# Adaptive-norm products on four column tiles, tanh in place of silu and sigmoid, and a wider spread of fillers in a two-branch attention layer

## The chip, the cores and the metric

The kernel runs on one core of one Trainium2 chip. The metric is device time in microseconds (us) from start to end of one launch; the program gives the median of several runs. TensorE (PE in the profile) does the matmuls, VectorE (DVE), ScalarE (ACT) and GpSimd (POOL) do the elementwise work, and SyncE (SP) issues nearly all DMAs.

## What is computed

One encoder layer is applied to two independent sequences ("prompt", group 0, and "sample", group 1) of 1024 tokens with 1024 channels in float32. Both share all weights.

```python
mod = einsum(silu(c), w_ada) + b_ada            # [B, 3*1024]
shift, scale, gate = split(mod, 3)
h = rms_norm(x, norm_g) * (1 + scale) + shift
qa, ka, va, za, qb, kb, vb, zb, ga, gb = split(h @ w_in)   # 5376 columns
oa = gqa_attention(rope(rms(qa)), rope(rms(ka)), va) * silu(za)
ob = diff_attention(rope(rms(qb)), rope(rms(kb)), vb, lam)
ob = rms_norm(ob, subln_g) * (1 - lam_init) * silu(zb)
merged = sigmoid(ga) * (oa @ w_proj_a) + sigmoid(gb) * (ob @ w_proj_b)
out = x + gate * (merged @ w_out)
```

Branch A has 8 query heads of 64 on 2 key heads; branch B has 4 heads with two softmax maps each. `c` is one vector per group, so the product with `w_ada` has two rows only.

## The kernel before

Activations are kept transposed, 128 channels on the partitions, and the big products are made with operands split in a high and a low part of type fp32r (three products instead of one). A whole group is worked through before the next one.

**Start.** `start` (L338) loads the part of `w_ada` that makes shift and scale in eight tiles of 1 MB (`load_ada`, L244: 512 rows by 512 columns), group 0's `xT` in two halves of 512 tokens (`load_xT0`, 2 MB each) and the first projection weight, `kva_w` (1 MB, `early=True`). All of that goes through SP's queue in the order of the program text: two w_ada tiles, the first half of `xT`, three w_ada tiles, `kva_w`, three w_ada tiles, the second half of `xT`. `ada` (L293) runs four matmuls for each tile: the stationary operand is two columns of `silu(c)` (`cT`, [128, 8, 2]), the moving one 512 columns of `w_ada`, and all eight of a pair of tiles accumulate in two PSUM partitions. `ada_end` (L301) copies the two rows out, transposes them with the identity and adds the bias. `modulated` (L318) then makes the two parts of `h` for the first half. For the second half `squares` and `inv_rms` (L267) sum the squares over all channels with a matmul against ones, 8 chunks by 4 token tiles, in two passes each; `start_late` (L367) finishes that half from inside the head. `spread` puts its row of 1/rms into the one `ev` buffer, which the gates of `z_gen` use too.

**Head.** `head` (L957) makes k, v and the first half of q of branch A (`proj_tt`, L487: 24 matmuls of 256 columns for each of 8 token tiles), and lays gate products of `z_gen` (L668) between them. For group 0 it weaves 6 steps of `kva` with 3 of the gates, calls `late()`, and weaves 6 and 3 again.

**Gates.** `z_gen` makes za, zb, ga and gb: 24 matmuls of 512 columns for each [128, 512] block, one ACT copy out of PSUM into `ev`, one DMA to HBM (`zd`). There are 48 blocks a group. The silu is taken later in `gated_gen` (L848), where the block comes back beside the attention output (`od`); the sigmoid is taken in `merge_gen` (L892, L906).

**Attention.** `attention` (L808) gives out 32 units a group. A unit is four blocks of scores (L709, L710), a row maximum (L711, DVE), an exponential (L712, ACT), a 32x32 block transpose (L753, DVE) with four DMAs (L762) that finish it, and the product with the values (`a_values` L764 for branch A, two column tiles of 64 columns; `b_values` L780 for branch B, full width). All other work is woven between these steps as fillers. `weave` (L72) always takes a step from the stream with the smallest `steps done / steps given - lead`.

**Last head.** L1085 weaves the last head of branch B (44 steps, given as `LAST_ATT` = 48) with `fill()` (given as `LAST_FILL` = 28) and with `gated_gen` for the first three pairs of channel blocks (12 steps, `GATED_A` = -0.2, which makes it begin late). `fill` holds, for group 0, `gate_gen` (L427: the third part of `w_ada`, 16 matmuls with two stationary columns, each on a tile of 256 KB from the `st` pool of three), then the gate blocks that are left, and then ten of the sixteen steps of branch A's projection (`merge_gen`). After that come the rest of the projections and `out_gen`.

The framework places the instructions of each engine from a simulated timeline in order of priority, so the order on an engine is near the text's but not the same. A tile of a pool is any free one of its `bufs` buffers.

Of the kernel before, what the change touches and what calls it, by code (L numbers as in the profile page):

```python
# [20 lines left out]
P = 128  # L21
# [33 lines left out]
LAST_ATT, LAST_FILL = (48, 28)  # L55
# [4 lines left out]

SILU = 0
# [29 lines left out]
def kernel(ctx: ExitStack, tc: tile.TileContext, t: dict):  # L91
# [79 lines left out]
    nhalf = const.tile([P, 32], F32, name="nhalf")  # L171
    nc.vector.memset(nhalf, -0.5)


# [53 lines left out]
    ccol = const.tile([P, NCH, 2], F32, name="ccol")  # L228
# [5 lines left out]
    dma(ccol, t["c_col"])  # L234
# [23 lines left out]
    def added(sq):  # L258

        a, b = sq  # L260
        nc.vector.tensor_tensor(out=a[:, :2], in0=a[:, :2], in1=b[:, :2], op=ALU.add)
        nc.vector.tensor_tensor(out=a[:, 2:], in0=a[:, 2:], in1=b[:, 2:], op=ALU.add)
        nc.vector.tensor_tensor(out=a[:, :2], in0=a[:, :2], in1=a[:, 2:], op=ALU.add)
        nc.vector.tensor_tensor(out=a[:, 0], in0=a[:, 0], in1=a[:, 1], op=ALU.add)
        return [a[:, 0]]

    def inv_rms(sq):  # L267

        ps = gbank()
        for k in range(4):  # L270
            for i, x in enumerate(sq):
                nc.tensor.matmul(
                    ps[:, k : k + 1], x[:, k * P : (k + 1) * P], ones_c, start=(i == 0), stop=(i == len(sq) - 1)
                )
        ss = tiny.tile([P, 4], F32, tag="ss", name=nm("ss"))
# [17 lines left out]
    def ada(n, wt):  # L293
        hf, third, q = n // 4, n // 2 % 2, n % 2
        if q == 0:
            accs[n // 2] = gbank()[:2]
        acc = accs[n // 2]
        for c in range(4):
            nc.tensor.matmul(acc, cT[:, q * 4 + c], wt[:, c], start=(q == 0 and c == 0), stop=(q == 1 and c == 3))

    def ada_end(n):  # L301
        hf, third = n // 4, n // 2 % 2
        acc = accs[n // 2]
        row = halves2(ptile())[0][:2]
# [12 lines left out]

    def modulated(ht, hf, xT, cs):  # L318
        for c in cs:
            scale, shift = modc[:, 1, c, 0:1], modc[:, 0, c, 0:1]  # L320
            if c % 4 > 1:
                nc.scalar.activation(xT[c], xT[c], AF.Identity, scale=scale, bias=shift)
            else:
                nc.vector.tensor_scalar(
                    out=xT[c], in0=xT[c], scalar1=scale, scalar2=shift, op0=ALU.mult, op1=ALU.add
                )
            nc.scalar.activation(ht[hf][0][c], xT[c], AF.Copy)
            nc.vector.tensor_tensor(out=ht[hf][1][c], in0=xT[c], in1=ht[hf][0][c].bitcast(F32), op=ALU.subtract)
# [9 lines left out]
    def start(ht):  # L338
        nc.scalar.activation(cT, ccol, AF.Silu)
# [5 lines left out]
        wts += [load_ada(n) for n in range(2, 5)]  # L345
        kva_w.append(load_w(w_cols(w_in, (C_KA, 256)), early=True))
        wts += [load_ada(n) for n in range(5, 8)]
        xT.append(load_xT0(1))
        for n in range(8):
# [8 lines left out]
            if n == 4:  # L358
                split_early(kva_w[0])
                add_h(ht, 0, 0)  # L360
                modulated(ht, 0, xT[0], range(4))
        add_h(ht, 0, 1)
        modulated(ht, 0, xT[0], range(4, 8))
        rs = inv_rms([q[:, c] for q in squares(xT[1]) for c in range(4)])
        return lambda: start_late(ht, xT, rs)
# [31 lines left out]
    def load_tables_B():  # L397
# [19 lines left out]
        nc.vector.tensor_scalar(out=subg, in0=subg, scalar1=(1.0 - LAM_INIT) * math.sqrt(2 * HD), scalar2=None, op0=ALU.mult)  # L417
# [9 lines left out]
    def gate_gen():  # L427
        for half in range(2):
            acc = gbank()[:2]
            for k in range(NCH):  # L430
                st = spool.tile([P, 512], F32, tag="st", name=nm("st"))
                col = 2 * D + half * 512
                dma(st, w_ada[k * P : (k + 1) * P, col : col + 512])
                nc.tensor.matmul(acc, cT[:, k], st, start=(k == 0), stop=(k == NCH - 1))
                if k % 2:
                    yield 1
            row = rtile()[:2]
            nc.vector.tensor_copy(row, acc)
            ps = gbank()[:, :8].rearrange("p (c g) -> p c g", g=2)
            for c in range(4):  # L440
                nc.tensor.transpose(ps[:, c, :], row[:, c * P : (c + 1) * P], ident[:2, :2])
# [3 lines left out]
            )  # L445

# [39 lines left out]

    def proj_tt(ht, w, tt):  # L487
# [4 lines left out]
        for c in range(NCH):  # L492
            if c in CUTS:
                yield 1
            for lt, wi in ((hh, 0), (hh, 1), (hl, 0)):
                nc.tensor.matmul(ps, lt[c][:, sl], w[:, c, wi, :], start=(k == 0), stop=(k == 23))  # L496
# [54 lines left out]

    def behind(ins, other):
        dep = mybir.DependencyInfo(mybir.DependencyClass.NoSync, mybir.DependencyReason.DATA)
        tc.add_manual_dep(ins.ins, other.ins.name, dep)

    def together(calls):

        prev = None
        for call in calls:
            if prev is None:  # L560
                ins = call()
            else:
                with tc.high_priority(offset=TOP):
                    ins = call()
                behind(ins, prev)
            prev = ins
# [101 lines left out]
    def z_gen(ht, col, dst, i0, fn=AF.Copy):  # L668
        w = load_w(w_cols(w_in, (col, 256)))
        for hf in range(2):  # L670
            for e in range(2):
# [3 lines left out]
                for c in range(NCH):  # L675
                    if c in CUTS:
                        yield 1
                    for wi, rt in ((0, hh), (0, hl), (1, hh)):
                        nc.tensor.matmul(  # L679
                            ps, w[:, c, wi, e * P : (e + 1) * P], rt[c],  # L680
                            start=(k == 0), stop=(k == 23),
                        )
                        k += 1
                ev = mtile("ev", [P, 512], bufs=1)
                nc.scalar.activation(ev, ps, fn)  # L685
# [162 lines left out]
    def gated_gen(st, i, hf, oT):  # L848

        if i == 0 and hf == 0:  # L850
# [5 lines left out]
            nc.scalar.activation(row, ps, AF.Copy)  # L856
# [7 lines left out]
        for c in range(2):  # L864
# [4 lines left out]
            if i >= SILU:  # L869
                nc.scalar.activation(z, z, AF.Silu)  # L870
# [21 lines left out]
    def merge_gen(st, br, oT, mT):  # L892

        for half in range(2):
            w = load_w_proj(br, half)
            for hf in range(2):
# [3 lines left out]
                for d in range(4):  # L900
                    dt_ = half * 4 + d
                    if d % 2 == 0:
# [3 lines left out]
                        nc.scalar.activation(gg, gg, AF.Sigmoid)  # L906
# [12 lines left out]
                    if br:  # L919
                        mh, ml = (mT[hf][dt_ // 2][:, d % 2, i, :] for i in range(2))  # L920
                        nc.vector.tensor_tensor(out=g, in0=ps, in1=g, op=ALU.mult)
# [3 lines left out]
                    else:  # L925
                        nc.vector.tensor_tensor(out=md[:, d], in0=ps, in1=g, op=ALU.mult)
# [30 lines left out]
    def head(g, st, zs, late):  # L957
# [64 lines left out]
    def z_item(st, i):  # L1022
        ht = st["ht"]
        fn = AF.Silu if i < SILU else AF.Copy
        if i < 2:
            return z_gen(ht, C_ZA + i * 256, st["zd"], i * 2, fn)
        if i < 4:
            return z_gen(ht, C_ZB + (i - 2) * 256, st["zd"], i * 2, fn)
# [118 lines left out]
```

## Time and profile before

| | |
|---|---|
| median of 3 runs (lowest to highest) | 1966.65 us (1964.79 to 1967.43) |
| the profiled execution: time, span | 1970.28 us, 1968.4 us |
| granted TensorE clock, mean | 0.983 |
| DVE, ACT, POOL busy | 1110.0, 861.2, 723.6 us |
| moved by DMA | 295.03 MB, mean 150 GB/s |

The span runs from the first to the last instruction. "Busy" adds up the instructions' own times; matmuls are pipelined, so PE can be busy and still run below its rate. A row of a timeline gives start, duration, engine, line, operation, output and inputs, count, and in brackets the idle time before it with what ended that. A row of a group gives busy time, mean ns of one, and idle time before. A row of windows gives the busy time of each engine in a stretch, then the granted clock, the DMA engines' busy share and GB/s.

### The profile page before, as it was taken

The numbers are of one execution on the slowest core, as the hardware profiler recorded it, in microseconds if no ns is written. First come the engines' busy times: TensorE is split into PE (matmuls) and PEld (weight loads), VectorE is DVE, ScalarE is ACT, GpSimd is POOL, SyncE is SP. The second block draws the span as 40 slices with busy tenths as digits, with TensorE's granted clock in tenths as the row PEclk, the third lists the DMA queues.
The fourth block names the chain that finished last, engine by engine and source line by source line (L and its number), as shares of the span: only waits on it lengthen the run. The fifth ranks groups of instructions, "written<-read, shape, count | busy, mean of one in ns | idle before, by whom it ended". The sixth has DMA issues, their size and how long they took to land.

```text
span 1968.4 us, 29657 instructions
## 1 busy us (share of the span) xinstructions
PE 1900.2 (97%) x10466; PEld 1574.4 (80%) x10466; DVE 1110.0 (56%) x1570; ACT 861.2 (44%) x1653; POOL 723.6 (37%) x1008
## 2 busy tenths in 40 slices
PE   8899999999999998899999999999999999999999
PEld 3788778888888984778889788888888798877887
DVE  5557762444667466647464667444447735665641
ACT  4434442444445344754323445333445524567410
POOL 2463431433465251221236544124456616412110
PEclk9899999999999999999999999999999999999999
DMA  8125674546243335875641567655524423567531
GB/s 313 47 73 159 186 204 135 161 123 201 79 136 111 100 86 173 248 236 192 206 157 41 141 190 194 176 161 147 159 78 137 114 74 92 169 204 270 168 102 54
DMA packets 269011, 295.03 MB, mean 150 GB/s; under 512 B 35264, under 2 KB 217664, under 8 KB 268864
## 3 DMA queue, kind: packets, MB, share of 16 engines
q1 hardware_dynamic: 268864, 293.15, 49.9%
q8 instruction: 83, 1.36, 0.3%
q14 instruction: 64, 0.52, 0.1%
HBM read 133.59 MB, written 42.01 MB: 89 GB/s over the span
## 4 chain that ended last, share of the span: by engine, by line
PE 81%; DMA 6%; ACT 3%; POOL 3%; DVE 3%; issue 2%; SPq 2%; ACTq 0%; POOLq 0%; DVEq 0%
PE f L679 21%; PE f L496 19%; PE f L915 6%; PE a L768 6%; PE f L944 5%; PE s L709 5%; PE s L710 5%; PE s L944 4%; PE a L785 4%; PE s L915 2%; DMA row<-zd 1%; SPq L762 1%; DMA st<-in_w_in_dram 1%; PE f L547 1%; DMA q<-p 1%
## 5 line engine op out<-in xcount | busy, mean ns | idle before, releaser
L679 PE MATMUL f<-u,w 128*128 128x512 f32 x2232 | 579.3, 398 | 1.7 <-ACT w L178 1.2
L496 PE MATMUL f<-w,u 128*128 128x256 f32 x3456 | 483.6, 286 | 2.5 <-ACT ev L685 1.6
L679 PEld LDWEIGHTS f<-u,w 128*128 128x128 f32 x2232 | 411.4, 190 | 85.3 <-issue 2.7
L496 PEld LDWEIGHTS f<-w,u 128*128 128x128 f32 x3456 | 456.3, 192 | 24.1 <-issue 2.3
L711 DVE TENSOR_REDUCE m<-s 128x1 f32<-128x1024 f32 x256 | 310.2, 1219 | 240.6 <-PE s L710 238.5
L712 ACT ACTIVATE p<-s,m 128x1024 f32<-128x1024 f32 x256 | 285.1, 1114 | 241.3 <-DVE m L711 208.8
L180 POOL TENSOR_TENSOR w<-st,w 128x512 fp32r<-128x512 f32 x168 | 220.9, 1332 | 456.4 <-ACT w L178 410.9
L753 DVE STREAM_TRANSPOSE p<-p 128x1024 f32<-128x1024 f32 x192 | 237.3, 1240 | 70.3 <-ACT p L712 61.7
L514 POOL TENSOR_TENSOR rs<-ss,nhalf 128x4 f32<-128x4 f32 (+1 forms) x112 | 110.0, 982 | 329.9 <-DVE ss L513 275.2
L710 PE MATMUL s<-u,sw 128*128 128x512 f32 x512 | 206.2, 403 | 0.0
L178 ACT ACTIVATE w<-st 128x512 fp32r<-128x512 f32 x196 | 114.6, 626 | 136.0 <-DMA st<-in_w_in_dram 79.7
L915 PE MATMUL f<-u,w 128*128 128x512 f32 x552 | 134.6, 398 | 4.4 <-ACT ev L685 3.7
L785 PE MATMUL a<-q,u 128*128 128x256 f32 x512 | 130.2, 393 | 7.3 <-DMA q<-p 5.5
L915 PEld LDWEIGHTS f<-u,w 128*128 128x128 f32 x552 | 104.7, 192 | 26.8 <-ACT ev L685 3.9
L709 PE MATMUL s<-u 128*128 128x512 f32 x256 | 111.2, 434 | 12.2 <-ACT p L712 12.0
L550 DVE TENSOR_TENSOR u<-f,u 64x256 fp32r<-64x256 f32 (+1 forms) x196 | 80.4, 411 | 71.3 <-ACT u L549 66.4
L768 PE MATMUL a<-q,u 128*64 128x256 f32 x1024 | 117.7, 382 | 0.8 <-DMA q<-p 0.8
L785 PEld LDWEIGHTS a<-q,u 128*128 128x128 f32 x512 | 99.0, 198 | 23.8 <-issue 7.8
L710 PEld LDWEIGHTS s<-u,sw 128*128 128x128 f32 x512 | 98.3, 192 | 17.4 <-issue 0.8
L709 PE MATMUL s<-u,u 128*128 128x512 f32 x256 | 104.7, 410 | 4.3 <-ACT p L712 3.4
L944 PE MATMUL f<-u,w 128*128 128x512 f32 x456 | 105.6, 389 | 0.0
L508 ACT ACTIVATE row<-f 128x256 f32<-128x256 f32 (+1 forms) x112 | 41.1, 367 | 146.1 <-PE f L496 135.5
(169 smaller groups left out, 2140.9 us busy)
## 6 DMA issues: line engine op xcount, KB each, us to landing
q<-p SPq DMA_DIRECT2D x768, 128.0 KB, 2.6
st<-in_w_in_dram SPq DMA_DIRECT2D x132, 256.0 KB, 3.1
zd<-ev SPq DMA_DIRECT2D x96, 256.0 KB, 2.5
sw<-u SPq DMA_DIRECT2D x256, 64.0 KB, 2.0
p<-zd SPq DMA_DIRECT2D x64, 256.0 KB, 3.8
u<-in_w_ada_dram SPq DMA_DIRECT2D x8, 1024.0 KB, 10.4
od<-oo SPq DMA_DIRECT2D x64, 128.0 KB, 2.4
st<-in_w_in_dram SPq DMA_DIRECT2D x64, 128.0 KB, 2.7
```

The lines of the kernel that those rows point to most:

```text
L180: e.tensor_tensor(out=wl, in0=st, in1=wh.bitcast(F32), op=ALU.subtract)
L496: nc.tensor.matmul(ps, lt[c][:, sl], w[:, c, wi, :], start=(k == 0), stop=(k == 23))
L679: nc.tensor.matmul(ps, w[:, c, wi, e * P : (e + 1) * P], rt[c], start=(k == 0), stop=(k == 23),)
L709: nc.tensor.matmul(s[:, sl], q, k[:, sl], start=True, stop=False)
L710: nc.tensor.matmul(s[:, sl], sw, k[:, sl], start=False, stop=True)
L711: nc.vector.tensor_reduce(out=m, in_=s, axis=AX.X, op=ALU.max, negate=True)
L712: nc.scalar.activation(pt.rearrange("p (j c a) -> p j c a", j=4, c=8), s.rearrange("p (c a j) -> p j c a", c=8, j=4), AF.Exp, bias=m, accu ...
L753: nc.vector.transpose(pt, pt)
L768: lambda k=k, m=m: nc.tensor.matmul(acc[(LO, HI)[m]], u["v"][:, k], pT[m][:, k], start=(k == 0), stop=(k == 7))
L785: nc.tensor.matmul(acc, u["v"][:, k], pT[:, k], start=(k == 0), stop=(k == 7))
L915: nc.tensor.matmul(ps, w[:, c, wi, d * P : (d + 1) * P], o[:, oi, :], start=(k == 0), stop=(k == 11))
L944: nc.tensor.matmul(ps, w[:, c, wi, e * P : (e + 1) * P], m[:, mi, :], start=(k == 0), stop=(k == 23))
```

## The change

- `ada` and `gate_gen` run their four chunks on four column tiles of 32 columns, one chunk on each, into four groups of 32 PSUM partitions; `cT` is padded with zeros so that 32 columns can be read from any chunk. `laid` replaces the transposes: a matmul of the copied rows against `pick`, which adds the four partial sums. `gate_gen` takes its weights in 1 MB tiles from the `u` pool, two DMAs of 512 KB each, and halves the gate at the end.
- In `start` all eight w_ada tiles stand ahead of `kva_w` and the second half of `xT`; `split_early` comes after the loop. The second half's squares are first added up on DVE (`added`), so that `inv_rms` needs one chunk instead of eight; it is called inside `late()`, behind the latest projection matmul. The first projection matmul is put behind the last `laid`, the first gate product behind the latest projection matmul.
- In the head of group 0, two rounds of `drain(6 steps of kva)`, `drain(3 steps of gates)` replace the weave.
- `z_gen` stores tanh of half the value; for za and zb a DVE instruction makes `(1 + tanh(z/2)) * z` from it and the PSUM bank. The silu and sigmoid of `gated_gen` and `merge_gen` go, the gating instruction after the projection becomes `(g + 1) * ps` in one DVE instruction, and the factors of one half go into `subg`, `rA` and `gatec`.
- `LAST_FILL` goes from 28 to 40.

```diff
-LAST_ATT, LAST_FILL = (48, 28)
+LAST_ATT, LAST_FILL = (48, 40)
...
-    cT = const.tile([P, NCH, 2], F32, name="cT")
+    cT = const.tile([P, NCH * 2 + 30], F32, name="cT")
+    nc.vector.memset(cT, 0.0)
+    pick = const.tile([P, 2], F32, name="pick")
+    for i in range(4):
+        nc.vector.tensor_copy(pick[i * 32 : i * 32 + 32], ident[i * 32 : i * 32 + 32, i * 32 : i * 32 + 2])
...
+    def across(acc, q, ws):
+        together([
+            lambda c=c: nc.tensor.matmul(
+                acc[c * 32 : c * 32 + 32], cT[:, (q * 4 + c) * 2 : (q * 4 + c) * 2 + 32], ws[c], start=(q == 0), stop=(q == 1),
+                tile_position=(0, c * 32),
+            )
+            for c in range(4)
+        ])
...
+    def laid(ps, row):
         for c in range(4):
-            nc.tensor.matmul(acc, cT[:, q * 4 + c], wt[:, c], start=(q == 0 and c == 0), stop=(q == 1 and c == 3))
+            picked[0] = nc.tensor.matmul(ps[:, c, :], row[:, c * P : (c + 1) * P], pick, start=True, stop=True)
...
-        for c in range(4):
-            nc.tensor.transpose(ps[:, c, :], row[:, c * P : (c + 1) * P], ident[:2, :2])
+        laid(ps, row)
...
         wts += [load_ada(n) for n in range(2, 5)]
+        wts += [load_ada(n) for n in range(5, 8)]
         kva_w.append(load_w(w_cols(w_in, (C_KA, 256)), early=True))
-        wts += [load_ada(n) for n in range(5, 8)]
...
-        rs = inv_rms([q[:, c] for q in squares(xT[1]) for c in range(4)])
-        return lambda: start_late(ht, xT, rs)
+        sq = squares(xT[1])
+        return lambda: start_late(ht, xT, inv_rms(added(sq, end), latest[0]))
...
-            acc = gbank()[:2]
-            for k in range(NCH):
-                st = spool.tile([P, 512], F32, tag="st", name=nm("st"))
-                dma(st, w_ada[k * P : (k + 1) * P, col : col + 512])
-                nc.tensor.matmul(acc, cT[:, k], st, start=(k == 0), stop=(k == NCH - 1))
-                if k % 2:
-                    yield 1
+            acc = gbank()
+            for q in range(2):
+                wt = chunks4(utile().bitcast(F32))
+                for c in range(0, 4, 2):
+                    rows = w_ada[(q * 4 + c) * P : (q * 4 + c + 2) * P, col : col + 512]
+                    dma(wt[:, c : c + 2], rows.rearrange("(c p) n -> p c n", p=P))
+                yield 1
+                across(acc, q, [wt[:, c] for c in range(4)])
+                yield 1
...
-                nc.scalar.activation(ev, ps, fn)
+                nc.scalar.activation(ev, ps, AF.Tanh, scale=0.5)
+                if silu:
+                    nc.vector.scalar_tensor_tensor(out=ev, in0=ev, scalar=1.0, in1=ps, op0=ALU.add, op1=ALU.mult)
...
-            if i >= SILU:
-                nc.scalar.activation(z, z, AF.Silu)
...
-                        nc.scalar.activation(gg, gg, AF.Sigmoid)
...
-                weave((islice(kva, 6), 6, 0.0), (islice(zs, 3), 3, 0.0))
+                drain(islice(kva, 6))
+                drain(islice(zs, 3))
                 if i == 0:
                     late()
```

More of the change, by code (lines that the diff above doesn't have):

```diff
@@ L170, with behind, together @@
     nc.vector.memset(ones_c, 1.0)
-    nhalf = const.tile([P, 32], F32, name="nhalf")
+    nhalf = const.tile([P, NTT], F32, name="nhalf")
     nc.vector.memset(nhalf, -0.5)
+    def behind(ins, other):
+        dep = mybir.DependencyInfo(mybir.DependencyClass.NoSync, mybir.DependencyReason.DATA)
+        tc.add_manual_dep(ins.ins, other.ins.name, dep)
+    def together(calls):
+        prev = None
+        for call in calls:
+            if prev is None:
+                ins = call()
+            else:
+                with tc.high_priority(offset=TOP):
+                    ins = call()
+                behind(ins, prev)
+            prev = ins
     def split_w(w, q, st):
@@ L256, in squares, with added @@
         return sq
-    def added(sq):
+    def added(sq, after=None):
         a, b = sq
-        nc.vector.tensor_tensor(out=a[:, :2], in0=a[:, :2], in1=b[:, :2], op=ALU.add)
+        ins = nc.vector.tensor_tensor(out=a[:, :2], in0=a[:, :2], in1=b[:, :2], op=ALU.add)
+        if after is not None:
+            behind(ins, after)
         nc.vector.tensor_tensor(out=a[:, 2:], in0=a[:, 2:], in1=b[:, 2:], op=ALU.add)
@@ L265, in added, with inv_rms @@
         return [a[:, 0]]
-    def inv_rms(sq):
+    def inv_rms(sq, after=None):
         ps = gbank()
@@ L484, in ht_gen @@
             yield 1
+    latest = [None]
     def proj_tt(ht, w, tt):
@@ L495, in proj_tt @@
             for lt, wi in ((hh, 0), (hh, 1), (hl, 0)):
-                nc.tensor.matmul(ps, lt[c][:, sl], w[:, c, wi, :], start=(k == 0), stop=(k == 23))
+                ins = nc.tensor.matmul(ps, lt[c][:, sl], w[:, c, wi, :], start=(k == 0), stop=(k == 23))
+                if latest[0] is None:
+                    behind(ins, picked[0])
+                latest[0] = ins
                 k += 1
```

67 lines of the change are left out of this document (31 added, 36 removed).

## The prediction

> **What bounds the kernel now.** I read the page first, then windows to find where TensorE loses time, then timelines of those stretches.
>
> ```profile
> PE 1900.2 (97%) x10466; PEld 1574.4 (80%) x10466; DVE 1110.0 (56%) x1570; ACT 861.2 (44%) x1653; POOL 723.6 (37%) x1008
> PE 81%; DMA 6%; ACT 3%; POOL 3%; DVE 3%; issue 2%; SPq 2%; ACTq 0%; POOLq 0%; DVEq 0%
> L679 PE MATMUL f<-u,w 128*128 128x512 f32 x2232 | 579.3, 398 | 1.7 <-ACT w L178 1.2
> ```
>
> TensorE is busy 97% of the span and makes 81% of the chain that ended last. So PE work taken away counts in full, and so does a PE stall; work taken from ACT or DVE counts only where PE waits for them. I looked for the stretches in which PE loses time all the same: the start and the last head of each group. The last row says that gate products almost never wait (1.7 us for 2232).
>
> **The start and the head.**
>
> ```profile
> 20.00:30.00 10.00, 10.00 (x36) 3.15 (x35) 2.73 (x7) 3.12 (x5) 3.89 (x5) 1.00 1.06 401
> 50.00:60.00 10.00, 10.00 (x41) 8.94 (x42) 1.56 (x6) 1.48 (x5) 1.59 (x2) 0.59 0.33 103
> 17.04 3.60 PE L299 MATMUL s<-u,cT 128*2 128x512 f32 x8 [0.20 <-DMA u<-in_w_ada_dram]
> 22.87 2.70 ACT L178 ACTIVATE w<-p 128x512 fp32r<-128x512 f32 x4 [7.22 <-DMA p<-in_w_in_dram]
> 29.43 10.46 PE L299 MATMUL f<-u,cT 128*2 128x512 f32 x24
> 37.22 4.25 ACT L255 ACTIVATE q<-u 128x512 f32<-128x512 f32 x8
> 41.69 1.70 PE L496 MATMUL f<-w,u 128*128 128x256 f32 x12
> 44.99 7.90 PE L272 MATMUL f<-ones_c,q 128*128 128x1 f32 x50
> 52.75 4.19 PE L679 MATMUL s<-u,w 128*128 128x512 f32 x9
> 64.00 2.00 DMA zd<-ev
> 77.55 3.62 PE L496 MATMUL f<-w,u 128*128 128x256 f32 x28 [1.65 <-ACT ev L685]
> 146.33 0.40 PE L709 MATMUL s<-u,u 128*128 128x512 f32 x1
> 17.49 1.23 DVE L263 TENSOR_TENSOR q<-q 128x1024 f32<-128x1024 f32 x1
> L376 ACT ACTIVATE u<-u,modc 128x512 f32<-128x512 f32 x8 | 5.6, 719 | 1.0 <-DVE u L373 0.9
> L377 ACT ACTIVATE u<-u 128x512 fp32r<-128x512 f32 x8 | 4.8, 622 | 0.0
> ```
>
> Columns of a windows row: stretch, its length, PE, PEld, DVE, ACT, POOL busy, clock, DMA share, GB/s. Until about 40 us the DMA engines are full at 0.40 MB/us. The third w_ada tile lands at 17.0. Yet PE ends its last w_ada product only at 39.9, 24 in a row without a wait: there the products are late, not the loads. Then come 64 sums of squares (L272), fifty of them in one 7.9 us block, and the dense work begins at 52.75 at a clock of 0.59. The second half's `h` is ready at 77.55; it waited for `ev`, which a gate's DMA held until 66.
>
> With the change a tile's products take about a quarter, so `ada` follows the loads. The eighth tile, now ahead of `kva_w`, lands at 17.0 + 5 x 1.05 MB / 0.40 = 30.1; `kva_w` at 32.7 (before, its last quarter by 24.9); the second half of `xT` at 38, as before, since the bytes ahead are the same. Working on from there by rows: `ada_end` to 33; `modulated` for four chunks to 38 (2 x 0.72 + 4 x 0.62 us of ACT and a last DVE subtraction); projections from about 36, dense work after. The second half: squares to 42.3 (4.25), additions to 47 (three of 1.23 and a half one), a short `inv_rms`; two projections and the first gate block end at about 50, its `ev` is free after tanh, the added DVE instruction and the 2.0 of its DMA, at 54; then 8 x (0.72 + 0.62) = 10.7 of ACT and the first copy: ready at 66 instead of 77.5. That is 11 us; PE by itself gains 52.75 - 36 - 2.8 (the 23 projection matmuls it had done) = 14. I take **-10**, bounds 0 (the ACT work of the second half fills the gap) and -14. Waiting longer for `kva_w` costs nothing, as h is ready later still. The padding and `pick` are small DVE copies ahead of the first load's landing; at nothing.
>
> **The gate products of the last head (group 0).**
>
> ```profile
> 748.77 2.74 PE L434 MATMUL f<-st,cT 128*2 128x512 f32 x6
> L434 PE MATMUL f<-st,cT 128*2 128x512 f32 x32 | 15.3, 592 | 2.4 <-DMA st<-in_w_ada_dram 2.4
> 169.88 3.60 PE a L768 x32
> 525.35 3.46 PE a L785 x16
> ```
>
> A float32 matmul is two records; 32 records for 16 matmuls, at 10.46/24 = 0.436 us each, are 13.9 us. What column tiles give is in the last two rows: sixteen matmuls on two tiles of 64 columns (branch A) take 3.60 us, eight full-width ones of as many columns take 3.46. Two run at a time, and changing into tiles and back costs 0.14 at most. Four tiles are in no row; bounds are 13.9 (serial) and 13.9/4 + 4 x 0.14 = 4.0. I take the lower one, since the two-tile row shows 1.92 of 2. `laid` is 8 records like L272 in place of 4 transposes, some 0.6 us more for each half: 1.2 together. Net **-9** (+1 to -9).
>
> The Trainium skill ("TensorE: Matmul & The Clock Gate", Part 3) gives 2.38 times for three column tiles and 3.07 for four row tiles; at 3.07 the products would take an estimated 4.5 us. The two-tile row is nearer to the ideal than that; the term would be -8.2 instead of -8.7, which I round to -9.
>
> The PE waits for these loads (2.4) should go too, as 512 KB pieces come ahead into `u` buffers: **-2**, bounds -2.4 and +5 (no `u` buffer free while the eight of `h` are held).
>
> **ACT in the two last heads.**
>
> ```profile
> L870 ACT ACT_TABLE_LOAD x20 | 25.7, 1283 | 16.3 <-DMA row<-zd 16.1
> L906 ACT ACTIVATE p<-p 128x1024 f32<-128x1024 f32 x32 | 33.8, 1059 | 40.1 <-DMA p<-zd 37.1 <-DVE u L926 1.8 <-DVE q L885 1.0
> L712 ACT ACT_TABLE_LOAD x13 | 16.7, 1283 | 0.2
> L906 ACT ACT_TABLE_LOAD x8 | 10.3, 1283 | 8.2 <-DMA p<-zd 8.1
> 770.61 1.28 ACT L870 ACT_TABLE_LOAD   x1
> 771.90 0.63 ACT L870 ACTIVATE row<-row 128x512 f32<-128x512 f32 x1
> 772.55 1.28 ACT L712 ACT_TABLE_LOAD   x1
> 824.27 1.01 PE L797 MATMUL f<-ones_c,at 128*128 128x1 f32 x4 [3.83 <-ACT ev L685]
> 825.14 11.24 PE L679 MATMUL f<-u,w 128*128 128x512 f32 x39
> 848.08 0.65 PE L880 MATMUL f<-ident,ssB 128*128 128x128 f32 x4 [2.75 <-ACT ev L685]
> 1754.38 0.55 PE L709 MATMUL s<-u 128*128 128x512 f32 x1 [2.13 <-ACT p L712]
> 1766.42 0.50 PE L709 MATMUL s<-u 128*128 128x512 f32 x1 [2.01 <-ACT p L712]
> 1782.92 8.03 PE L915 MATMUL f<-u,w 128*128 128x512 f32 x22 [3.69 <-ACT ev L685]
> ```
>
> The silu of a block makes ACT load its table and then the exponential's again: 1.28 + 0.63 + 1.28 us (770.6 to 773.8). All 41 loads of these three rows (52.7 us), the sigmoids (33.8) and 32 silus (32 x 0.63 = 20) lie there: 106 us of ACT that goes, while tanh takes the place of a copy of the same shape. PE waits for that ACT: 3.83 + 2.75 in group 0, 2.13 + 2.01 + 3.69 in group 1. After a stop the clock is low: 39 matmuls took 11.24 us where 24 take 5.44 in the dense stretches (0.227 each, 8.8), 2.4 lost; 22 took 8.03 where 5.0 would do, 3.0 lost. That is 9.0 for group 0 and 10.8 for group 1, bounds of 0 and -20 together. I take **-8 and -8**: the waits have ACT alone as their last releaser, but DMAs stand close behind.
>
> `LAST_FILL`: at 28 to 48, the 44 attention steps carry 26 of the 36 fill steps of group 0 (8 of the gate, 18 of blocks) and of the 34 of group 1 (24 + 10), and the merge's ten come after. At 40 to 48 all are laid beside attention. The PE work is the same, so by itself nothing. It asks for the gated blocks sooner, at step 31 of attention instead of 44; with no silu in their way I leave it in the -16.
>
> **What is added: a second reader of the PSUM bank.**
>
> ```profile
> L685 ACT ACTIVATE ev<-f 128x512 f32<-128x512 f32 x93 | 55.2, 594 | 91.5 <-PE f L679 78.0 <-DMA q<-p 3.6 <-issue 3.4
> L949 DVE SCALAR_TENSOR_TENSOR q<-f,gatec,q 128x512 f32<-128x512 f32 x19 | 14.2, 748 | 46.1 <-PE f L944 46.1
> L711 DVE TENSOR_REDUCE m<-s 128x1 f32<-128x1024 f32 x256 | 310.2, 1219 | 240.6 <-PE s L710 238.5
> ```
>
> 32 blocks of za and zb get a DVE instruction of about 0.75 us, which waits for the tanh and for what stands ahead on DVE (a reduction of 1.22, at times two). The bank and `ev` are then held for 0.6 + 2.4 + 0.75 = 3.8 us instead of 0.6. A block's matmuls take 24 x 0.227 = 5.4 and three `f` banks rotate, so mostly it is hidden; other evictions queue a little behind it. I take **+3**, bounds 0 and +63 (32 x 1.97 all on PE).
>
> **Sum.** -10 - 9 - 2 - 8 - 8 + 3 = -34. The profiled execution took 1970.28 us (span 1968.4), giving 1936.3; it stands 3.6 above the median, so against the median 1966.65 - 34 = **1932.7 us**.
>
> **Rivals.**
>
> - *Transfers take ACT's place* (0.16). In group 0's last head blocks of `zd` and `od` also end waits, and the DMA engines are full (second row below). Then only a few of the 16 come: -34 + 16 = -18, 1948.7.
>
> ```profile
> 741.75 6.66 PE L785 MATMUL a<-q,u 128*128 128x256 f32 x16 [5.46 <-DMA q<-p]
> 840.00:870.00 30.00, 26.58 (x129) 21.66 (x127) 14.35 (x24) 16.92 (x23) 6.96 (x6) 1.00 0.86 295
> ```
>
> - *The head stays bound by the second half's `h`* (0.12): the 10.7 us of ACT queue with gates, weights and evictions, and the start gains nothing at the end: -24, 1942.7.
> - *The tiles don't overlap* (0.04): PE keeps 13.9 us and the start follows the products: about -21, 1945.7. Against it, the branch A row.
> - *All of it comes* (0.15): -14 - 9 - 2 - 20, no cost for the second reader, and the stall at 741.75 (first row above: 5.5 us for a block, then 16 matmuls in 6.66 where 3.46 do, 8.7 together) disappears in the new order: -54, 1912.7.
> - *Slower: the second reader stalls PE* (0.08). Place: the gates of za and zb in the head and first two attention phases. Price up to 32 x 1.97 = 63, so -37 + 63 = +26, 1993. It decides from a mean stall of 37/32 = 1.2 us a block, about one reduction. Against it: 1.7 us of waits over 2232 matmuls now.
> - *Slower: tanh isn't in the exponential's table* (0.03). Then each of 96 blocks pays two loads, 246 us of ACT. The 41 loads of before lost 20 us of PE, 0.5 each; 192 lose 96: 1933 + 96 = 2029. The Trainium skill ("ScalarE: Activation LUTs", Table sets: the hidden batching unit) lists tanh among `exp_and_others`; by that rule there is no load, but no row of this trace has a tanh.
>
> **How the numbers follow.** The forecast gets 0.40; 0.02 is left for a new order of work that eats the gain. The range must hold 8 in 10: from near the "all of it" case to the weaker ones, 1911 to 1952, leaving out the slower cases and parts of the ends. A change of 0.2% (3.9 us) is what this measurement can tell. Faster: 0.40 + 0.16 + 0.12 + 0.04 + 0.15 = 0.87; slower 0.10; within 0.03.
>
> **What would show it.** The w_ada products end near 31 us; the second half's first projection (tile 4) starts near 66 and attention near 136 instead of 146.3. The gate products of the last head take about 4 us. The 41 table loads go. No PE wait above 2 us ends with `ev` L685 in the last heads, and ACT is under half busy there (16.92 of 30 us in the row above). The new DVE rows wait under 2 us and the za and zb matmuls still wait for nothing. I am wrong if table loads stand in the attention stages, if PE waits for DVE behind `ev`, or if DMA rows replace the ACT rows with the same sums.

## The result, and the profile after

The changed kernel takes 1941.01 us (median of 4 runs, 1939.89 to 1944.48) against 1966.8 for the kernel before beside it: a ratio of 0.9863, interval 0.9847 to 0.9879, so 25.8 us faster. Forecast was 1932.7, 34 us faster, with a range of 1911 to 1952.

The page of the changed kernel, its totals and two groups:

```profile
span 1942.7 us, 29466 instructions
PE 1867.0 (96%) x10434; PEld 1566.8 (81%) x10434; DVE 1137.7 (59%) x1613; ACT 760.3 (39%) x1548; POOL 724.5 (37%) x1008
L709 PE MATMUL f<-u,w 128*128 128x512 f32 x2256 | 588.3, 397 | 2.5 <-ACT w L192 1.0
L802 PE MATMUL a<-q,u 128*64 128x256 f32 x1024 | 119.2, 385 | 5.7 <-DMA q<-p 5.7
```

ACT lost 101 us (861.2 to 760.3) and DVE gained 28, but PE lost 33 us of busy time, and the time went down by 26. The gate products (L709, formerly L679) still wait for almost nothing: the added reader does not show there. The 5.7 us at the value products (L802) will matter below.

Groups of the same trace, with each shape apart:

```profile
L717 ACT ACTIVATE ev<-f 128x512 f32<-128x512 f32 x94 | 55.9, 595 | 107.9 <-PE f L709 90.3 <-DMA zd<-ev 6.2 <-issue 5.6
L719 DVE SCALAR_TENSOR_TENSOR ev<-ev,f 128x512 f32<-128x512 f32 x30 | 20.3, 677 | 19.9 <-ACT ev L717 19.7
L378 ACT ACT_TABLE_LOAD x1 | 1.3, 1283 | 6.0 <-DMA cT<-in_c_col_dram 6.0
L452 ACT ACT_TABLE_LOAD x1 | 1.3, 1283 | 0.0
```

These last two are the only table loads left. The tanh of 94 recorded blocks costs what the copy cost (595 ns against 594), so the Trainium skill's list of `exp_and_others` ("ScalarE: Activation LUTs", Table sets: the hidden batching unit) holds here: tanh and exponential alternate through all of attention without a load.

The start, PE's timeline:

```profile
16.46 1.93 PE L324 MATMUL s<-u,cT 128*32 128x512 f32 x8 [2.59 <-DMA u<-in_w_ada_dram]
18.38 1.87 PE L291 MATMUL f<-ones_c,q 128*128 128x1 f32 x8
32.19 1.93 PE L324 MATMUL f<-u,cT 128*32 128x512 f32 x8
39.28 7.63 PE L539 MATMUL f<-w,u 128*128 128x256 f32 x48
70.37 2.20 PE L539 MATMUL f<-w,u 128*128 128x256 f32 x17
135.45 0.39 PE L743 MATMUL s<-u,u 128*128 128x512 f32 x1
```

The w_ada products end at 34.1 (39.9 before), dense work begins at 39.3 (52.8), the second half's first projection stands at 70.4 (77.6) and attention at 135.45 (146.33).

The gate products of group 0's last head, the same view:

```profile
743.23 1.92 PE L324 MATMUL f<-u,cT 128*32 128x512 f32 x16
746.55 0.95 PE L336 MATMUL f<-pick,row 128*128 128x2 f32 x8
747.43 1.92 PE L324 MATMUL f<-u,cT 128*32 128x512 f32 x16
```

3.84 us in all, where 32 records one after the other would take 13.9 by the 0.436 us each of the start before, and took 14.1 in c1 (below): four column tiles overlap 3.6 times. They wait for no load.

To see where the rest comes from, I counted, for each trace, the matmul records of the big products at their dense rate, and compared the times at which a kernel and the kernel before have done the same work. Each column is what a stage gained (-) or lost (+), in us; g0 and g1 are the groups, "last" their last head with the projections after it, "g1 up to it" all of group 1 ahead of its last head. All rows are one profiled execution each, against the profiled execution of before, which was 3.6 above its median.

```
run                    start   g0 first  g0      g0     g1 up   g1
                       + head  phase     middle  last   to it   last    sum
after                  -10.9   +4.4      +0.1   -21.0   +5.5    -3.9   -25.8
a1_fill28               -9.7   +4.1      -1.2    -9.8   +5.7   -10.6   -21.5
a2_no_second_reader    -11.3   -0.8      +0.0   -23.4   +1.9    -2.2   -35.8
a3_tanh_late           -11.3   -0.3      -0.3   -20.7   -1.5    +1.8   -32.3
a4_old_gates           -11.4   -0.8      -0.1    -5.8   +0.7   +16.5    -0.9
a5_late_fill_40_28      -7.8   -0.8      +1.7   -17.2   +2.2    -1.4   -23.3
a6_fill_40_28          -10.3   +3.9      -1.6   -22.8   +2.0    -9.2   -38.0
a8_late_in_group_0      -8.2   -0.8      +1.4   -19.1   +1.9   -10.1   -34.9
b1_before_fill40        -0.9   +0.0      -1.2    +5.0   -1.5   +16.3   +17.7
b2_before_tanh          +0.0   +4.9      +0.1    -8.8   +4.8   -10.9    -9.9
b3_before_gate_tiles    +3.1   +0.6      -0.9    -1.8   +1.0    -0.9    +1.1
c1_serial_products      -5.9   +4.4      -0.2    -9.6   +4.2    -3.7   -10.8
c2_old_load_order       -9.9   +4.4      -0.5   -22.9   +0.6    -2.5   -30.8
```

How far may one execution be trusted? a3 and a5 run the same program up to the end of group 0, and stand at -32.6 and -24.1 there; after and c2 have the same program in all of group 1 and differ by 4.9 in the stages ahead of its last head; b3 has the start and head of the kernel before and stands at +3.1 there. So a single entry tells little below some 5 us; what follows rests on entries that come back in several rows, and on the timed ratios. "After" itself has four differences to explain: the start, the +4.4, the -21.0 and the -3.9.

### The profile page after: what moved, and what is told of

The parts are those of the page before. It is cut to its first block, busy times and chain, and to the rows that moved or that the text cites. A ratio compares the mean times of both kernels' runs of the same rounds, so it can differ in the third digit from the quotient of the medians.

```text
span 1942.7 us, 29466 instructions
## 1 busy us (share of the span) xinstructions
PE 1867.0 (96%) x10434; PEld 1566.8 (81%) x10434; DVE 1137.7 (59%) x1613; ACT 760.3 (39%) x1548; POOL 724.5 (37%) x1008
## 5 line engine op out<-in xcount | busy, mean ns | idle before, releaser
L709 PE MATMUL f<-u,w 128*128 128x512 f32 x2256 | 588.3, 397 | 2.5 <-ACT w L192 1.0
L709 PEld LDWEIGHTS f<-u,w 128*128 128x128 f32 x2256 | 414.5, 189 | 87.4 <-issue 3.1
L946 PE MATMUL f<-u,w 128*128 128x512 f32 x552 | 136.8, 398 | 4.0 <-DVE u L957 3.0
L802 PE MATMUL a<-q,u 128*64 128x256 f32 x1024 | 119.2, 385 | 5.7 <-DMA q<-p 5.7
L743 PE MATMUL s<-u 128*128 128x512 f32 x256 | 108.5, 424 | 10.7 <-ACT p L746 9.9
L744 PEld LDWEIGHTS s<-u,sw 128*128 128x128 f32 x512 | 97.6, 191 | 17.7 <-issue 0.8
L802 PEld LDWEIGHTS a<-q,u 128*64 128x64 f32 x1024 | 75.3, 138 | 43.9 <-issue 11.4
L977 PE MATMUL f<-u,w 128*128 128x512 f32 x456 | 105.6, 389 | 0.0
```

The costliest lines, as they stand in the source:

```text
L709: ins = nc.tensor.matmul(ps, w[:, c, wi, e * P : (e + 1) * P], rt[c], start=(k == 0), stop=(k == 23),)
L743: nc.tensor.matmul(s[:, sl], q, k[:, sl], start=True, stop=False)
L744: nc.tensor.matmul(s[:, sl], sw, k[:, sl], start=False, stop=True)
L802: lambda k=k, m=m: nc.tensor.matmul(acc[(LO, HI)[m]], u["v"][:, k], pT[m][:, k], start=(k == 0), stop=(k == 7))
L946: nc.tensor.matmul(ps, w[:, c, wi, d * P : (d + 1) * P], o[:, oi, :], start=(k == 0), stop=(k == 11))
L977: nc.tensor.matmul(ps, w[:, c, wi, e * P : (e + 1) * P], m[:, mi, :], start=(k == 0), stop=(k == 23))
```

## The experiments

Each ratio is to the kernel before on the same chip, with its interval. Kernels named a and c start from the changed kernel, b from the kernel before.

**Fillers as before.**

```diff
-LAST_ATT, LAST_FILL = (48, 40)
+LAST_ATT, LAST_FILL = (48, 28)
```

> The changed kernel with LAST_FILL put back to 28. Theory (fillers run out): at 40 the merge's ten steps are spent beside attention, and the chain of the last gated blocks then waits for its DMAs with nothing to cover it; in group 1 the changed kernel had gained 32 us up to work that stands at 1767 us and had 25.8 left at 1800. With 28 these 6 us come back: about 1935 us, and no PE loss between the end of attention and the second projection in group 1. Rival (the spread pays): attention's last head has too few fillers at 28, and PE waits for ACT and DVE there: 1945 us or more.

Measured: 1949.34 us, 0.9900 (0.988 to 0.9921), 7 us behind the changed kernel (0.0037 x 1967). The theory missed and the rival held: group 0's last head gives back 11 of its 21 us, group 1's gains 7. PE's waits in group 0's last head, total, times, longest:

```profile
PE s L743 <- ACT p L746: 6.7, 5, 2.9
```

The changed kernel has 1.8 in this row. With fewer fillers between attention's steps, scores stand waiting for the exponential of the step before: the number is worth a great deal, with opposite signs in the two groups (the theory was right for group 1).

**Without the second reader.** za and zb are stored as tanh only; the factor z is left out.

```diff
-                if silu:
-                    nc.vector.scalar_tensor_tensor(out=ev, in0=ev, scalar=1.0, in1=ps, op0=ALU.add, op1=ALU.mult)
```

> The changed kernel without the DVE instruction that multiplies za and zb into the tanh: what is stored for these blocks is the tanh alone, so that factor of the result is left out; all else is the same. Theory (the second reader costs more than the +3 that I gave it): against equal matmul work the changed kernel loses 4.4 us in the first attention phase of group 0 and 7.9 us in the head and first phase of group 1, where za and zb are made; without the instruction these 12 us go, about 1929 us. Rival (the losses there come from another order of the same work): 1937 to 1945 us, with losses of the same size in the same phases, at other places.

Measured: 1931.43 us, 0.9807 (0.9793 to 0.9822). The DVE instruction costs 0.0056 x 1967 = 11 us; by the two intervals this is good to some 4 us. The theory held. PE's waits in group 0's first phase, in the changed kernel:

```profile
PE a L802 <- DMA q<-p: 3.1, 2, 2.3
PE f L539 <- DVE ev L719: 1.1, 1, 1.1
PE f L709 <- DVE ev L719: 0.8, 1, 0.8
```

and in this one:

```profile
PE f L709 <- POOL w L194: 0.6, 1, 0.6
```

The waits for the bank itself are 1.9 us; the larger ones stand at a place that never touches that bank. The timeline of the changed kernel shows how:

```profile
221.98 1.25 DVE L787 STREAM_TRANSPOSE p<-p 128x1024 f32<-128x1024 f32 x1
...
223.15 0.65 DVE L719 SCALAR_TENSOR_TENSOR ev<-ev,f 128x512 f32<-128x512 f32 x1
...
223.72 1.21 DVE L745 TENSOR_REDUCE m<-s 128x1 f32<-128x1024 f32 x1
...
224.86 1.22 DVE L787 STREAM_TRANSPOSE p<-p 128x1024 f32<-128x1024 f32 x1
...
225.51 3.76 PE L802 MATMUL a<-q,u 128*64 128x256 f32 x32 [2.25 <-DMA q<-p]
```

In these rows DVE takes one instruction after the other. Between tanh's end at 222.0 (it began at 221.42 and takes 0.60) and 223.15 the new instruction waited behind a transpose; it then stood ahead of the next row maximum, and that ahead of the transpose whose blocks the `q<-p` DMAs carry to the value products.

**The second reader put off.** The gates of za and zb are stored raw; tanh and the DVE instruction follow in `gated_gen`.

```diff
-                nc.scalar.activation(ev, ps, AF.Tanh, scale=0.5)
                 if silu:
-                    nc.vector.scalar_tensor_tensor(out=ev, in0=ev, scalar=1.0, in1=ps, op0=ALU.add, op1=ALU.mult)
+                    nc.scalar.activation(ev, ps, AF.Copy)
+                else:
+                    nc.scalar.activation(ev, ps, AF.Tanh, scale=0.5)
...
+                nc.scalar.activation(z, z, AF.Tanh, scale=0.5)
+                nc.vector.scalar_tensor_tensor(out=o, in0=z, scalar=1.0, in1=o, op0=ALU.add, op1=ALU.mult)
```

> The changed kernel with za and zb stored as they are (one ACT copy), and the tanh and the multiplication taken in the gating of the last head, in place, on blocks that are in SBUF. The same DVE and ACT instructions, at another place and with no PSUM bank held. Theory (second reader): the 12 us of the early phases come back, and 16 blocks a group cost 0 to 5 us in the last heads: 1929 to 1936 us. Rival (DVE and the DMA chain bind the last heads): what is won early is lost there, 1939 us or more. Rival (order): 1937 to 1945 us without a pattern.

Measured: 1939.19 us, 0.9846 (0.9831 to 0.986), no better than the changed kernel by the intervals. The theory missed and the first rival held: group 0's first phase loses nothing, but group 1's last head gives it back (+1.8 against -3.9). PE's waits there:

```profile
PE f L951 <- DVE u L962: 6.2, 3, 3.1
```

The changed kernel has 1.7 in the like row (L957). The work is cheap in neither place.

**Silu and sigmoid as before, all else changed.**

```diff
-                nc.scalar.activation(ev, ps, AF.Tanh, scale=0.5)
-                if silu:
-                    nc.vector.scalar_tensor_tensor(out=ev, in0=ev, scalar=1.0, in1=ps, op0=ALU.add, op1=ALU.mult)
+                nc.scalar.activation(ev, ps, AF.Copy)
...
+            nc.scalar.activation(z, z, AF.Silu)
...
+                        nc.scalar.activation(gg, gg, AF.Sigmoid)
```

> The changed kernel with the gates of before: copies stored, silu and sigmoid taken in the last heads, factors of one half taken out. Theory (the tanh part is worth its ACT stalls of about 14 us in the last heads less 12 us for the second reader): 1943 us, faster in the first phases and slower in the last heads. Rival (the tanh part carries the gain): 1953 us or more. If the table loads were never on the path: 1930 us.

Measured: 1968.92 us, 0.9999 (0.9988 to 1.001). The rival held, and not the theory of 1943. The 11 us of the start are there and all lost by the end, 16.5 in group 1's last head. PE's waits there:

```profile
PE s L740 <- ACT p L743: 8.8, 2, 7.8
```

The wait of 7.8 us ends at 1753.7, with this exponential (last row):

```profile
1746.83 1.28 ACT L936 ACT_TABLE_LOAD   x1 [2.16 <-DMA p<-zd]
...
1751.14 1.28 ACT L743 ACT_TABLE_LOAD   x1
1752.43 1.11 ACT L743 ACTIVATE p<-s,m 128x1024 f32<-128x1024 f32 x1
```

It stands behind a sigmoid (L936), for whose block ACT waits 2.16 us, a silu (L900) and three table loads: with the fillers spread, these fall into attention. So tanh is worth 26.7 us within the whole change (0.0136 x 1967).

**The kernel before with the fillers spread.**

```diff
-LAST_ATT, LAST_FILL = (48, 28)
+LAST_ATT, LAST_FILL = (48, 40)
```

> The kernel before with LAST_FILL 40 and nothing else. Theory (with silu and its table loads in the way, the merge laid beside attention waits for gated blocks): slower, as the changed kernel with the old gates lost 16 us in group 1's last head: 1975 to 1990 us. Rival (the spread by itself pays): 1965 us or less.

Measured: 1990.2 us, 1.011 (1.0083 to 1.0138): 22 us slower, at the upper end of the theory's range, 16 of them in group 1's last head as in a4, where this row stands:

```profile
PE s L709 <- ACT p L712: 9.4, 2, 8.4
```

**The kernel before with tanh alone** (`z_gen`, `gated_gen`, `merge_gen` and the factors of one half as in the change).

```diff
-                nc.scalar.activation(ev, ps, fn)
+                nc.scalar.activation(ev, ps, AF.Tanh, scale=0.5)
+                if silu:
+                    nc.vector.scalar_tensor_tensor(out=ev, in0=ev, scalar=1.0, in1=ps, op0=ALU.add, op1=ALU.mult)
...
-                nc.scalar.activation(z, z, AF.Silu)
...
-                        nc.scalar.activation(gg, gg, AF.Sigmoid)
```

> The kernel before with the tanh gates and nothing else (old products, old start, LAST_FILL 28). Theory: about -16 in the last heads (ACT stalls) and +10 to +12 in the phases where za and zb are made: 1963 to 1966 us. Rival (the tanh needs the spread to pay at all, or the second reader eats it): 1969 us or more. If the ACT stalls are worth more than I took: 1957 us or less.

Measured: 1960.38 us, 0.9955 (0.9938 to 0.9973). That is better than the theory (1963 to 1966) and short of the 1957 expected if the stalls were worth more than forecast. The last heads give -8.8 and -10.9, the first phase takes +4.9 back, group 1's early part as much.

**The kernel before with the gate products of the last head on four tiles** (`gate_gen` alone).

```diff
-                nc.tensor.matmul(acc, cT[:, k], st, start=(k == 0), stop=(k == NCH - 1))
...
+                across(acc, q, [wt[:, c] for c in range(4)])
```

> The kernel before with the gate products of gate_gen on four column tiles, loaded into u buffers, and nothing else (LAST_FILL 28, silu and sigmoid as before). Theory (filler work taken from the last head pays only when other work moves in, as it does at 40): attention there waits for its own DVE and ACT chain, and nothing or at most 3 us is won: 1966 to 1969 us. Rival (PE work counts in full, as I predicted): 1958 to 1961 us.

Measured: 1967.45 us, 1.0001 (0.999 to 1.0012). Ten us of PE work went and nothing came of it, as the theory said. PE's waits in that last head:

```profile
PE s L731 <- ACT p L734: 10.7, 5, 4.5
PE a L807 <- DMA q<-p: 7.5, 2, 5.7
```

The same two rows in the kernel before:

```profile
PE s L709 <- ACT p L712: 0.5, 2, 0.4
PE a L785 <- DMA q<-p: 5.5, 1, 5.5
```

By these rows the slow products were what PE did while the attention steps waited for their exponentials; without them PE waits instead. Silu and table loads need not be the reason: a1 has none of them, has 28 fillers too, and waits 6.7 us for exponentials there.

**The changed kernel with all w_ada products one after the other** (start and gate products; `laid` is made of transposes again).

```diff
-            accs[n // 2] = gbank()
+            accs[n // 2] = gbank()[:2]
...
-                acc[c * 32 : c * 32 + 32], cT[:, (q * 4 + c) * 2 : (q * 4 + c) * 2 + 32], ws[c], start=(q == 0), stop=(q == 1),
-                tile_position=(0, c * 32),
+                acc, cT[:, (q * 4 + c) * 2 : (q * 4 + c) * 2 + 2], ws[c],
+                start=(q == 0 and c == 0), stop=(q == 1 and c == 3),
```

> The changed kernel with the w_ada products of the start and of the last head one after the other on two columns, as before; loads, order, sums of squares, tanh and LAST_FILL 40 as changed. Theory (tiles matter at both places): the start's products end near 39 us instead of 33 and the head loses 4 to 8 of its 11 us; group 0's last head loses 8 to 10: 1953 to 1959 us. Rival for the start (the short sum of squares and the order are what counts): attention begins within 2 us of the changed kernel. Rival for the last head (the products are hidden there): under 3 us lost.

Measured: 1961.48 us, 0.9971 (0.9961 to 0.9981), 21 us behind the changed kernel and a little behind the theory's 1953 to 1959. The start gains 5.9 instead of 10.9, and group 0's last head 9.6 instead of 21.0. The two make 16 of the 21 us; the table doesn't place the rest. Here the same 10 us of PE work that b3 removed for nothing are worth 11. The table tells what makes the difference; group 0's last head, in us:

| | `LAST_FILL` 28 | `LAST_FILL` 40 |
|---|---|---|
| silu, gate products one after the other | 0 (before) | +5.0 (b1) |
| silu, gate products on tiles | -1.8 (b3) | -5.8 (a4) |
| tanh, gate products one after the other | -8.8 (b2) | -9.6 (c1) |
| tanh, gate products on tiles | -9.8 (a1) | -21.0 (after) |

At 28 the tiles give 1 to 2 us, at 40 they give 11, with silu and its loads as much as with tanh. The timed ratios agree: a4 is 0.0111 x 1967 = 22 us under b1, of which the new start makes 10.5 by the table; a1 is 11 us under b2 (0.0055), of which the start makes 9.7.

**The changed kernel with the loads in their old order.**

```diff
-        wts += [load_ada(n) for n in range(5, 8)]
         kva_w.append(load_w(w_cols(w_in, (C_KA, 256)), early=True))
+        wts += [load_ada(n) for n in range(5, 8)]
```

> The changed kernel with the loads of the start in the order of before: the projection weight ahead of the last three w_ada tiles. Theory (the last w_ada tile is what the head waits for): one weight of 1.05 MB ahead of it at 0.4 MB/us makes the products end 2.6 us later, and the head begins attention 1 to 3 us later: 1942 to 1944 us. Rival (order of loads decides the head): 5 us or more lost. Rival (the chain of the second half hides it): no difference.

Measured: 1939.45 us, 0.9861 (0.9845 to 0.9878), the same as the changed kernel. The theory of 1942 to 1944 missed; the rival of no difference held. By c1 and c2 the start's 11 us are some 5 for the tiles and none for the order of the loads. What is left, some 6, would fall to the added-up squares and the written order of head and projections; no run has these by themselves, and the eight runs with the changed start and loads read from -7.8 to -11.4 there.

**40 in group 0 and 28 in group 1**, with the second reader put off (a5), as the change has it (a6), and put off in group 0 alone (a8).

```diff
-LAST_ATT, LAST_FILL = (48, 40)
+LAST_ATT, LAST_FILL = (48, (40, 28))
...
-        weave((until_next(att), LAST_ATT, 0.0), (fill(), LAST_FILL, 0.0), (gates(), 12, GATED_A))
+        weave((until_next(att), LAST_ATT, 0.0), (fill(), LAST_FILL[g], 0.0), (gates(), 12, GATED_A))
```

> The kernel with the tanh taken late (run a3), with LAST_FILL 40 in group 0 and 28 in group 1. At equal matmul work a3 led the kernel before by 34 us when group 1's last head began and by 32 after it; with 28 the changed kernel gained 10.6 there instead of 4.4. Theory (in group 1 the spread takes the cover from the last gated blocks): 34 + 10 = 44 us under the kernel before, about 1925 us. Rival (the gain at 28 in group 1 came with another order in that run alone): 1936 to 1942 us, as a3.

> The changed kernel with LAST_FILL 40 in group 0 and 28 in group 1, all else as changed. Theory: it keeps the gain of group 0's last head (19 us, where 28 left 8) and takes group 1's with 28 (10.6 instead of 4.4): about 1936 us on a chip where the kernel before takes 1969. Rival: 1941 to 1946 us.

> Run a6 (LAST_FILL 40 in group 0, 28 in group 1) with the tanh of za and zb taken late, in the gating, in group 0 alone. The first attention phase of group 0 lost 3.9 to 4.9 us in all four runs with the second reader of the bank and nothing in the five without; a3's late tanh cost group 0's last head nothing measurable and group 1's 5 to 8. Theory (second reader): about 4 us under a6, 1930 us where the kernel before takes 1969. Rival (what a3 and a5 showed is the spread between executions): 1934 us, as a6.

Measured: a5 1939.35 us, 0.9852 (0.9822 to 0.9882); a6 1934.17 us, 0.9821 (0.9799 to 0.9842); a8 1937.07 us, 0.9847 (0.9832 to 0.9862). **a6 beats both kernels**, by a single number. Group 1's last head gives -9.2 there and -10.1 in a8, as in a1 and b2, which have 28 too; with 40 it gave -3.9, -2.2, -3.7 and -2.5 (after, a2, c1, c2). a5 (-1.4) has 28 but puts the second reader off in group 1 too, as a3 does, which at 40 stands at +1.8: in both the late work is worse by 6 to 8 us in that stage. (a5's profiled execution was also the longest of four, 1935.5 to 1946.9.) Putting the second reader off in group 0 alone saves the first phase (-0.8 against +3.9), as meant, and the time does not fall. Of the three, only a6 came out as its theory said.

What the changed kernel does in group 1 there is in its chain of work that ended last:

```profile
1769.78 5.47 DMA q<-zd
...
1784.26 3.82 DMA st<-in_w_proj_b_dram
...
1790.34 6.71 PE f L946 x29
```

At 40 the last head has used up the projection steps, and the blocks that come back from HBM and the next weight stand in the chain. The windows of these last 40 us of the stage, first the changed kernel:

```profile
1765.00:1805.00 40.00, 36.79 (x169) 30.00 (x168) 21.40 (x34) 7.17 (x13) 8.77 (x9) 0.96 0.70 225
```

then a6, 7 us ahead of it where these windows begin and 12 where they end:

```profile
1755.00:1795.00 40.00, 38.95 (x181) 31.59 (x180) 21.66 (x31) 5.55 (x10) 7.85 (x6) 1.00 0.69 245
```

12 matmul records more and a clock of 1.00 against 0.96 in the same time: PE had work left.

## Why the prediction was right, and where it was not

The sign and the range held; the sum was 8 us too hopeful. By its number alone 1941.0 lies nearest to the rival *the head stays bound* (1942.7), which did not come true: attention begins at 135.45. Point by point:

- **The start, -10: right in size, with some luck** (-10.9; attention at 135.45, forecast 136). The products ended 3 us later than forecast, at 34.1: the last of them stand behind a `laid` at 30.40, for which DVE copies the rows until then. In a6, with the same start, PE waits for that copy and ends at the same time:

```profile
30.38 1.87 PE L336 MATMUL f<-pick,p 128*128 128x2 f32 x8 [2.81 <-DVE p L342]
```

  The second half's first projection stood 4 us later than forecast, and that was made up before attention, which the working did not foresee. c2 shows that one reason given was not needed: the products could follow the loads in either order. c1 shows that the tiles carry about half.
- **Gate products of the last head, -9: right in this kernel, wrong in its reason.** 3.84 us against a forecast of 4.0, no wait for loads (-2, right), and c1 puts their worth at 11. But the step "PE work taken away counts in full" is refuted by b3: in the kernel before, the same removal is worth nothing. It counts here because `LAST_FILL` went to 40: at 28 it gains 1 to 2 us with tanh too (a1 against b2), at 40 it gains 11 without tanh too (a4 against b1).
- **ACT in the last heads, -8 and -8: as forecast or better in both groups.** b2 alone gives -8.8 and -10.9. The loads are gone, no PE wait of over 2 us ends with `ev` there, and ACT is busy 30% (12.59 of 42 us) where it was 76% (32.11) in the same stretch before:

```profile
800.00:842.00 42.00, 36.28 (x154) 29.16 (x153) 25.51 (x33) 32.11 (x45) 12.64 (x12) 0.92 0.82 253
800.00:842.00 42.00, 37.69 (x171) 30.20 (x170) 31.46 (x43) 12.59 (x22) 9.65 (x10) 1.00 0.87 285
```

- **`LAST_FILL`, "by itself nothing": the step that failed.** Alone it costs 22 us (b1). In the changed kernel it gains 11 in group 0 (after against a1) and loses 5 to 7 in group 1. That its cover and its costs depend on what stands in ACT's queue was seen ("no silu in their way") but given no price. That group 0's last head made -21.0 where -19 (9 + 2 + 8) was summed is luck: tanh gives 9 of it, and the other 12 come from the tiles and the spread together, of which either alone gives about 1 beside tanh. In group 1 the spread took back most of what tanh gave: -3.9 is left of -10.6 (a1). The rival *transfers take ACT's place* came true in that one stage, as far as its chain shows.
- **The second reader, +3: mis-sized.** It measured 11 us (a2). The first phase of group 0 shows +3.9 to +4.9 in all six runs that have it there, and -0.8 to +0.6 in all seven that haven't. The working looked at who waits for the PSUM bank, and there it was right (1.9 us in that phase, and the new rows wait 0.66 us on average). What it left out is who stands behind the instruction on DVE: row maximum, transpose, the DMAs after it, and the value products.
- **The sum** -34 against -25.8: of the 8 us, 8 are the second reader (11 for 3) and 4 group 1's last head; the start and group 0's last head gave some 3 more than forecast.

Left open: whether the bank held longer or the queue on DVE makes most of the second reader's 11 us. An ACT copy of the bank ahead of tanh, which would free it at once, was not tried. Open too is why the changed kernel loses 5.5 us in group 1 ahead of its last head, where c2, with the same program there, loses 0.6; why the tiles and the spread pay only together in group 0's last head (the waits for exponentials at 28, 6.7 us in a1 and 10.7 in b3, fit, but no run varies them alone); and why a3 and a8 do not gain what their first phase saves, beyond the DVE waits of a3.

## What to carry to other kernels

A busy engine's work counts in full only where no other chain ends almost as late: b3 took 10 us from an engine that was busy 97% and gained nothing, and the same edit gained 11 where more fillers lay beside attention. Two parts of a change can be worth nothing apart and much together, so vary them in pairs before a price is put on either. Price an added instruction by what stands behind it on its own engine, not only by who waits for its result. Fillers are a stock to be shared between the stage that hides them and the stage after: look at both ends, and for each group by itself.

## What the hardware showed that was not expected

- In the start, one set of tile products (8 records) took 1.93 us, in the last head two sets took 1.92; yet the windows show a granted clock of 1.00 in both places:

```profile
20.00:30.00 10.00, 10.00 (x46) 3.65 (x45) 7.03 (x10) 0.60 (x1) 4.66 (x4) 1.00 1.05 404
740.00:750.00 10.00, 8.64 (x60) 4.62 (x60) 5.91 (x12) 4.30 (x9) 2.65 (x9) 1.00 0.13 39
```

  The eight sums of squares (L291) right behind one such set took 1.87 us. In c1, with the products one after the other, its timeline has them at full rate:

```profile
16.30 3.59 PE L324 MATMUL s<-u,cT 128*2 128x512 f32 x8 [0.27 <-DMA u<-in_w_ada_dram]
19.83 0.41 PE L336 MATMUL f<-ident,p 2*128 2x2 f32 x4
20.16 1.05 PE L291 MATMUL f<-ones_c,q 128*128 128x1 f32 x8
```

  So this work ran at about half rate, though PE shows no idle time from 16.46 to 34.1 us, and the clock column does not tell it. It also changes from one execution to the next: a6 has the same start, and there a set took 1.06 us from 25 us on:

```profile
25.22 1.06 PE L324 MATMUL f<-u,cT 128*32 128x512 f32 x8
```

  The Trainium skill ("TensorE: Matmul & The Clock Gate", Part 1) describes such a gate, half the clock until PE has been busy for some 3.4 us. The half rate agrees; the clock column doesn't, nor does the 17.7 us that PE stayed busy at that rate, and what set the rate is not shown. It cost little here: the projections begin at 39.1 to 39.4 us in all eight runs with this start.
- Four column tiles of 32 overlapped 3.6 times (13.9 us to 3.84) with float32 operands of 512 columns; in c1, one after the other, they took 7.03 us for each half. The Trainium skill (the same page, Part 3) gives 2.38 for three column tiles and 3.07 for four row tiles.
